# Column sums, stores and a last stage in block products: a transformer block in split fp32

## The chip, the cores and the metric

The kernel runs on one core of a Trainium2 chip. The time is that of the device for one execution, in microseconds (us). The engines are TensorE (PE in the rows; PEld its loading of weights), VectorE (DVE), ScalarE (ACT), GpSimd (POOL) and SyncE (SP). A name with a q at its end (SPq, POOLq) is an engine's own sequencer, which issues DMAs in order.

## What is computed

One layer of a transformer block for 512 tokens of width 2048, all in fp32:

```python
sh_a, sc_a, g_a, sh_f, sc_f, g_f = jnp.split(jax.nn.silu(c) @ ada_w[l] + ada_b[l], 6, axis=-1)
h = modulate(rms_norm(x, norm_mix[l]), sh_a, sc_a)
proj = h @ w_in[l]
...
x = x + g_a[:, None, :] * (jnp.concatenate([y_conv, y_attn], axis=-1) @ w_out[l])
h = modulate(rms_norm(x, norm_ffn[l]), sh_f, sc_f)
x = x + g_f[:, None, :] * ((jax.nn.silu(h @ ffn_w1[l]) * (h @ ffn_w3[l])) @ ffn_w2[l])
```

y_conv is a short convolution over three slices of proj, y_attn an attention over compressed, selected and near keys. The feed forward is 5632 wide, 44 blocks of 128. The vectors of the first line are 2048 long each; shift, scale and gate of the feed forward are its last three.

## The kernel before

**Numbers.** Each fp32 operand is split in a rounded part (hi, by a copy on ScalarE) and a remainder (lo, by a subtraction on VectorE), and a product is three matmuls: hi by lo, lo by hi, hi by hi (mm3, L96). A block of weights is loaded by SyncE, split, and then multiplied.

**The order.** The program is written as steps, and a scheduler places the instructions on each engine by it; woven generators (weave, L102) put steps of one work between steps of another. An engine runs its row in order, and so does a queue of DMAs.

**Column sums.** ada (L169) makes 512 columns of silu(c) @ ada_w: 16 pieces of the matrix, 128 x 512 (256 KB) each, are loaded by SyncE into a ring, and VectorE adds each, scaled, to acc (L185, one instruction of 128 x 512 a piece). ada_cols (L188) turns the sum into a column for shift or scale. In the token blocks (203 to 317 us) no sum is made. Beside the convolutions (317 to 700) ffn_cols (L792) makes six of the eight columns of the feed forward, one behind each convolution, out of a ring of two pieces. In the w_out stage (700 to 860; four column blocks n, L842) the ring has three buffers of two pieces; there stand, each in one piece, the sums of g_a for n + 1 and the last two columns. The gate of the feed forward, four rows, is made by gate_rows (L1106) inside the up stage: its loads are on GpSimd's queue, its sums (L1116) on VectorE, one step each third product.

**x2.** The result of w_out plus x is stored to memory as xd (L859), and read back in the end.

**Up stage** (920 to 1823 us). Each of 44 blocks u of 128 hidden columns: the first two plain, the other 42 as seven block products instead of eight (Strassen's method in Winograd's form; a product is 8 matmuls 512 wide, L922, and 8 of 256, L924). blocks (L894) loads four weight blocks by SyncE and, for the sum of two of them, loads the first again into t (or t2) and lets an accumulating DMA on GpSimd's queue add the second. More sums are made on VectorE (L1011). more and take (L929, L933) bring products together in d. The finished block is stored to memory (gd) by GpSimd (store, L974). begin starts the loads of a block five products ahead of its first.

**Down stage** (from 1823 us). Forty of the 44 hidden blocks in four groups b of ten, again as seven products of five units j, each unit 12 matmuls 512 wide (L1255). k_load (L1171) reads hidden blocks back on GpSimd's queue; a_parts (L1176) sums and splits them (ghi L1203, glo L1204); w_load (L1209) loads weights some units ahead, w_sum makes the sums for products 6 and 4 on VectorE (L1232, L1234), w_split splits (L1240), evict (L1258) adds products to y2. The last four blocks come as a plain tail (L1313 to the end): y2 times gate, plus xd, then 192 matmuls, and per tile a multiply, an add and a store.

Of the kernel before, what the change touches and what calls it, by code (L numbers as in the profile page):

```python
# [17 lines left out]
P = 128  # L18
# [51 lines left out]
def block_kernel(ctx: ExitStack, tc: tile.TileContext, a: dict, out: bass.AP):  # L70
# [98 lines left out]
    def ada(ring, width, c0, n, bias=False):  # L169
# [16 lines left out]
        return acc  # L186
# [203 lines left out]

    qk = ExitStack()
# [112 lines left out]
    def compress():  # L504
        per = cpool.tile([CMP_BLOCK, 2, HD], F32, name="per")
# [51 lines left out]
        b1 = cpool.tile([P, 256], F32, name="b1")  # L557
        hid = cpool.tile([P, 256], F32, name="hid")
# [21 lines left out]
        hrep = cpool.tile([P, 2, R, 32], F32, name="hrep")  # L580
        nc.gpsimd.memset(hrep, 0.0)
        for g in range(NKV):
# [4 lines left out]
            for h in range(2):  # L587
                nc.tensor.matmul(pv[:, :HD], hrep[:, h].rearrange("p r n -> p (r n)"), cw2[:, 1, h, :],
                                 start=h == 0, stop=h == 1)
# [20 lines left out]
    weave(token_blocks(), before_attention(), 1.5)  # L610
# [179 lines left out]
    wring = pool("aring", 2, stack=at_)  # L790

    def ffn_cols(ring_, width, j):  # L792

        m, j = 1 - j % 2, j // 2
        ada_cols(aux, ada(ring_, width, (3 + m) * D + j * 512, 512), 1, m, 4 * j, 4)

    def convs():
        for c in range(8):
            yield from conv(c)
            if c < 6:  # L800
                ffn_cols(wring, 512, c)
# [41 lines left out]
    for n in range(4):  # L843
# [3 lines left out]
        ada_bcast(aux, ga, acc_g)  # L847
        if n < 3:
            acc_g = ada(aring, 1024, 2 * D + (n + 1) * 512, 512, bias=True)
        pst = [main() for _ in range(NT)]  # L850
        for _ in token_block(w_out, n * 512, yT, every[8:] + every[:8], pst):
            pass
# [6 lines left out]
        nc.gpsimd.dma_start(xd[n], x2s[n])  # L859
        if n < 3:  # L860
            if n < 2:
                ffn_cols(aring, 1024, 6 + n)
            x2_turned(n)
# [88 lines left out]
    def h_sums(step):  # L952
# [15 lines left out]
        elif step == 4 * PLAIN - 1:  # L968
            h_parts(3, A[0, 1], 0, HK)
            hst.close()  # L970
            zone[1] = pool("raw2", 8, stack=ust, side="right")

    def store(f, g):
        (nc.gpsimd if f + 1 < NU else nc.scalar).dma_start(gd[f], g)  # L974
# [92 lines left out]

    order, late = [], None
# [37 lines left out]
    def gate_rows():  # L1106

        acc, raw = (accp.tile([P, 512], F32, tag="acc", name="acc") for _ in range(2))
        for n in range(4):
            c0 = 5 * D + n * 512  # L1110
            nc.gpsimd.memset(acc, 0.0)
            nc.gpsimd.dma_start(acc[0:1, :], a["ada_b"][:, c0:c0 + 512])
            for k in range(KC):
                nc.gpsimd.dma_start(raw, ada_v[:, k, c0:c0 + 512])
                yield
                nc.vector.scalar_tensor_tensor(acc, raw, cT[:, k:k + 1], acc, op0=ALU.mult, op1=ALU.add)  # L1116
            ps = aux()
            nc.tensor.matmul(ps[0:1, :], ones[:, 0:1], acc, start=True, stop=True)
            nc.scalar.copy(raw[0:1, :], ps[0:1, :])
            nc.gpsimd.dma_start(gfd[:, n * 512:(n + 1) * 512], raw[0:1, :])  # L1120

    gate = gate_rows()
# [8 lines left out]
    for n, s in enumerate(order):  # L1131
# [3 lines left out]
        if n + 5 < len(order):  # L1135
            begin(order[n + 5]["u"])
# [3 lines left out]
        if n >= 4 * PLAIN and n % 3 == 0:  # L1140
            next(gate, None)
# [9 lines left out]
    GC, HN = 5, D // 2  # L1151
    NG = FF // P // (2 * GC)
    tail = range(NG * 2 * GC, FF // P)
    PRODUCTS = (1, 5, 6, 3, 7, 2, 4)
    krp = pool("kraw", 1)
    gpp = pool("gparts", 3)
    ep = pool("e", 1)
    wz = pool("wz", 6)
    tz = pool("tz", GC)
    yp = pool("y2", 1)  # L1160
    y2 = yp.tile([P, NT, D], F32, name="y2")
    gf = yp.tile([P, D], F32, name="gf")
    tp = pool("tmp2", 2)
    kraw, W, A_, bank = {}, {}, {}, {}

    def k_load(b, half):

        fs = tail if b == NG else range((2 * b + half) * GC, (2 * b + half + 1) * GC)
        t = kraw[b, half] = krp.tile([P, GC, S], F32, tag=f"k{half}", name=f"k{half}")
        for j, f in enumerate(fs):  # L1170
            nc.gpsimd.dma_start(t[:, j, :], gd[f])  # L1171
# [6 lines left out]
    def a_parts_(b, p):  # L1178
        n = GC
# [100 lines left out]
    for n in range(-10, 0):  # L1280
        loads(n)
# [76 lines left out]
```

## Time and profile before

| | us |
|---|---|
| median of the runs (2299.56 to 2306.39) | 2303.61 |
| the profiled execution | 2297.38 |
| its span | 2295.6 |
| TensorE busy | 2197.4 |
| VectorE busy | 1758.1 |
| ScalarE busy | 989.5 |

The page gives busy time, the granted clock of TensorE (PEclk, 1.00 is full speed), the waits (engine line waited for: us, times, longest) and the chain that ended last. A wait names the engine that idled, its line and what released it. Lines are those of the kernel before; in the changed kernel they lie some 38 to 45 lower.

### The profile page before, as it was taken

To read this page: it belongs to the slowest core of one execution; us is meant where nothing else is said; L and a number is where in the kernel's file an instruction comes from. 1 tells how busy PE (TensorE), PEld (TensorE's weight loads), DVE (VectorE), ACT (ScalarE), POOL (GpSimd) and SP (SyncE) were. 2 spreads that over 40 slices of the span, in tenths; PEclk is the share of its full clock that TensorE was granted. 3 is DMA by queue.
4 is the path that set the end of the run, shared out by engine and by line. 5 is a ranking of instruction groups with operands and counts; after the bars stand their busy time and mean duration, and the time that the engine had idled before them with its cause. 6 is when DMAs were issued, how large, how long until landed. Compare 5 with 4: busy or idle time off the path is not lost. (4 is left out here: it accounts for less than half of the span.)

```text
span 2295.6 us, 30548 instructions
## 1 busy us (share of the span) xinstructions
PE 2197.4 (96%) x11401; PEld 1822.9 (79%) x11401; DVE 1758.1 (77%) x2577; ACT 989.5 (43%) x1554; POOL 263.9 (11%) x358
## 2 busy tenths in 40 slices
PE   7999999999999998999999999999999899999998
PEld 5788778787788776878888888888888777787776
DVE  6878478877756764968778788887878668888988
ACT  5235244555443232634444444444444354444441
POOL 5410000000000001010111111111010111101101
PEclk9999999999999999999999999999999999999999
DMA  9964455544435866397777777877776489576644
GB/s 325 363 215 135 158 180 168 173 127 143 120 118 202 277 231 179 112 217 170 181 201 182 196 193 198 214 183 179 175 175 157 160 250 266 164 219 215 168 136 160
DMA packets 432353, 435.20 MB, mean 190 GB/s; under 512 B 18132, under 2 KB 345016, under 8 KB 431052
## 3 DMA queue, kind: packets, MB, share of 16 engines
q1 hardware_dynamic: 358236, 303.38, 42.4%
q0 software_dynamic: 73824, 129.60, 23.5%
q8 instruction: 89, 1.46, 0.2%
q14 instruction: 60, 0.49, 0.1%
q10 hardware_dynamic: 144, 0.26, 0.0%
HBM read 413.25 MB, written 19.93 MB: 189 GB/s over the span
## 5 line engine op out<-in xcount | busy, mean ns | idle before, releaser
L910 ACT CAST whi<-raw 128x1024 fp32r<-128x1024 f32 x280 | 292.8, 1048 | 306.7 <-PE main L922 132.3
L922 PE MATMUL main<-hC,whi 128*128 128x512 f32 x1408 | 356.9, 395 | 9.2 <-DVE d L933 5.2
L915 DVE TENSOR_TENSOR wlo<-raw,whi 128x1024 fp32r<-128x1024 f32 x260 | 315.6, 1217 | 47.2 <-ACT whi L910 45.7
L922 PEld LDWEIGHTS main<-hC,whi 128*128 128x128 f32 x1408 | 253.6, 189 | 60.0 <-DVE d L933 7.3
L922 PE MATMUL aux<-hC,whi 128*128 128x512 f32 x1072 | 273.7, 398 | 13.0 <-DVE d L933 13.0
L922 PEld LDWEIGHTS aux<-hC,whi 128*128 128x128 f32 x1072 | 195.4, 191 | 51.9 <-DVE d L933 14.8
L924 PEld LDWEIGHTS main<-hC,wlo 128*128 128x128 f32 x1408 | 192.0, 190 | 13.8
L924 PE MATMUL main<-hC,wlo 128*128 128x256 f32 x1408 | 196.2, 282 | 0.0
L92 ACT CAST whi<-raw 128x1024 fp32r<-128x1024 f32 (+2 forms) x92 | 87.9, 959 | 230.9 <-PE main L100 143.5
L98 PE MATMUL main<-alo,whi 128*128 128x512 f32 x448 | 180.1, 402 | 1.4 <-DVE alo L346 1.4
L185 DVE SCALAR_TENSOR_TENSOR acc<-araw,cT,acc 128x512 f32<-128x512 f32 x184 | 137.7, 749 | 55.2 <-DMA araw<-in_ada_w 49.9
L99 PE MATMUL main<-ahi,wlo 128*128 128x512 f32 x448 | 176.6, 394 | 0.0
L100 PE MATMUL main<-ahi,whi 128*128 128x512 f32 x448 | 176.2, 394 | 0.0
L910 ACT CAST whi<-t 128x1024 fp32r<-128x1024 f32 x102 | 107.2, 1052 | 126.5 <-PE main L1255 32.3
L924 PEld LDWEIGHTS aux<-hC,wlo 128*128 128x128 f32 x1072 | 147.5, 192 | 11.1 <-DVE wlo L915 0.4
L98 PE MATMUL main<-wlo,ahi 128*128 128x512 f32 x384 | 152.7, 398 | 1.7 <-DVE t L856 1.6
L924 PE MATMUL aux<-hC,wlo 128*128 128x256 f32 x1072 | 150.9, 284 | 0.0
L100 PE MATMUL main<-whi,ahi 128*128 128x512 f32 x384 | 150.7, 393 | 0.0
L99 PE MATMUL main<-whi,alo 128*128 128x512 f32 x384 | 150.6, 392 | 0.0
L1011 DVE TENSOR_TENSOR raw<-raw 128x1024 f32<-128x1024 f32 x84 | 102.3, 1218 | 59.7 <-DMA raw<-in_ffn_w 59.5
L93 DVE TENSOR_TENSOR wlo<-raw,whi 128x1024 fp32r<-128x1024 f32 (+2 forms) x92 | 101.0, 1103 | 46.3 <-ACT whi L92 45.9
L1255 PE MATMUL main<-wlo,ghi 128*128 128x512 f32 x280 | 111.2, 399 | 14.0 <-ACT ghi L1203 7.4
(332 smaller groups left out, 4198.0 us busy)
## 6 DMA issues: line engine op xcount, KB each, us to landing
raw<-in_ffn_w SPq DMA_DIRECT2D x225, 512.0 KB, 5.0
w<-in_ffn_w SPq DMA_DIRECT2D x60, 512.0 KB, 5.2
araw<-in_ada_w POOLq DMA_DIRECT2D x56, 512.0 KB, 14.1
araw<-in_ada_w SPq DMA_DIRECT2D x112, 256.0 KB, 3.0
raw<-in_w_in SPq DMA_DIRECT2D x128, 192.0 KB, 2.7
t<-in_ffn_w SPq DMA_DIRECT2D x41, 512.0 KB, 6.4
t<-in_ffn_w POOLq DMA_DIRECT2D x41, 512.0 KB, 8.9
araw<-in_ada_w SPq DMA_DIRECT2D x40, 512.0 KB, 5.8
```

Source lines behind the costliest of these rows:

```text
L92: nc.scalar.copy(hi[:, :m], raw[:, :m])
L93: nc.vector.tensor_sub(lo[:, :m], raw[:, :m], hi[:, :m].bitcast(F32))
L98: nc.tensor.matmul(ps, lhs[0], rhs[1], start=first, stop=False)
L99: nc.tensor.matmul(ps, lhs[1], rhs[0], start=False, stop=False)
L100: nc.tensor.matmul(ps, lhs[0], rhs[0], start=False, stop=last)
L185: nc.vector.scalar_tensor_tensor(acc, w, s, acc, op0=ALU.mult, op1=ALU.add)
L910: nc.scalar.copy(hi, t)
L915: nc.vector.tensor_sub(lo, t, hi.bitcast(F32))
L922: nc.tensor.matmul(ps, wt[0][:, ks[k]], hC[p][:, k, :], start=first and k == 0, stop=False, skip_group_check=True)
L924: nc.tensor.matmul(ps[:, HS:], wt[1][:, ks[k]], hC[p][:, k, 0:HS], start=False, stop=last and k == HK - 1, skip_group_check=True)
L1011: nc.vector.tensor_add(to, x, y)
L1255: nc.tensor.matmul(ps[2 * t + c], x_[:, j, tok], w[:, cs], start=m == 0 and j == 0 and p in (1, 5, 2), stop=m == 2 and j == GC - 1 and p i ...
```

## The change

- **Column sums woven.** ada becomes a generator that gives way after each load. Twelve parts for the feed forward (eight columns of shift and scale, and the gate's four rows, ffn_part) are spread by beside: parts 0 to 2 in the token blocks (3.2 steps to one), 3 to 9 beside the convolutions (1.9), 10 and 11 in the last w_out block (2.5), and g_a's in the first three (1). gate_rows is gone from the up stage. Some tiles of the key compression share buffers, to make room for the ring.
- **x2 goes to the output.** It is stored to out itself, in pieces of 512 KB, and only tokens 256 to 511 of columns 0 to 1023 to xd.
- **Up stage.** Blocks are stored by SyncE in place of GpSimd; loads begin seven products ahead in place of five; five products before the end the second pool of weights (now its own stack) is closed, and the hidden blocks of the first down group are read.
- **Down stage.** All 44 blocks in block products, groups of 5, 6, 6, 5 units a product (22 units in each of seven products, no tail). The sum for product 4 is made by an accumulating DMA on GpSimd's queue, ten units ahead, the sum for product 6 by an add four units ahead; signs are turned in a_parts. In the last group finished blocks are scaled by the gate and added into out by six accumulating DMAs of 512 KB; the last product is done with xd, its last three units tile by tile.

The core of the diff:

```diff
-    def ada(ring, width, c0, n, bias=False):
+    def ada(ring, width, c0, n, got, bias=False):
...
                     nc.vector.scalar_tensor_tensor(acc, w, s, acc, op0=ALU.mult, op1=ALU.add)
-        return acc
+            yield
+        got.append(acc)
...
+    def ffn_part(ring_, width, j):
+
+        got = []
+        if j < 8:
+            m, j = 1 - j % 2, j // 2
+            yield from ada(ring_, width, (3 + m) * D + j * 512, 512, got)
+            ada_cols(aux, got[0], 1, m, 4 * j, 4)
+        else:
+            cs = slice((j - 8) * 512, (j - 7) * 512)
+            yield from ada(ring_, width, 5 * D + cs.start, 512, got, bias=True)
...
+            nc.gpsimd.dma_start(gfd[:, cs], got[0][0:1, :])
+        yield
...
-    weave(token_blocks(), before_attention(), 1.5)
+    early = ffn_parts(wring, 512, range(3))
+    weave(beside(token_blocks(), early, 3.2), before_attention(), 1.5)
...
+    later = ffn_parts(wring, 512, range(3, 10))
+    weave(beside(convs(), later, 1.9), attention_steps(), 0.68)
...
+        weave(token_block(w_out, n * 512, yT, every[8:] + every[:8], pst), side, 1 if n < 3 else 2.5)
...
-        nc.gpsimd.dma_start(xd[n], x2s[n])
+        for i in range(0, NT, 2):
+            to = xd[n] if n < 2 and i else \
+                out[0, i * P:(i + 2) * P, n * 512:(n + 1) * 512].rearrange("(i p) n -> p i n", p=P)
+            nc.gpsimd.dma_start(to, x2s[n][:, i:i + 2, :])
...
-        (nc.gpsimd if f + 1 < NU else nc.scalar).dma_start(gd[f], g)
+        (nc.sync if f + 1 < NU else nc.scalar).dma_start(gd[f], g)
...
-        if n + 5 < len(order):
-            begin(order[n + 5]["u"])
+        for m in (n + 6, n + 7) if n < 4 * PLAIN else (n + 7,):
+            if m < len(order) and (n >= 4 * PLAIN or m < 4 * PLAIN + 1):
+                begin(order[m]["u"])
...
-        if n >= 4 * PLAIN and n % 3 == 0:
-            next(gate, None)
+        if n == len(order) - 5:
+            zst.close()
+            krp = pool("kraw", 1, side="right")
+            for half in range(2):
+                k_load(0, half)
...
+        elif p == 4:
+            nc.gpsimd.dma_start(W[b, "t", j], block(1, 0), accum_op=ALU.add)
...
-            nc.vector.scalar_tensor_tensor(t, t, -1.0, W[b, 22, j], op0=ALU.mult, op1=ALU.subtract)
-        elif p == 4:
-            nc.vector.tensor_sub(t, W[b, 21, j], t)
+            t = W[b, "t", j]
+            nc.vector.tensor_add(t, t, W[b, 22, j])
...
+                if last and p in (3, 7, 2):
+                    nc.vector.scalar_tensor_tensor(y, y, -1.0 if c else 1.0, gf[:, cs], op0=ALU.mult, op1=ALU.mult)
+            if last and p in (3, 7, 2):
+                i = 2 * r + t
+                nc.gpsimd.dma_start(out[0, i * P:(i + 1) * P, c * HN:(c + 1) * HN], y2[i][:, c * HN:(c + 1) * HN],
+                                    accum_op=ALU.add)
...
-    AHEAD = {1: 4, 5: 9, 6: 10, 7: 7, 2: 7}
+    AHEAD = {1: 4, 5: 9, 6: 6, 7: 7, 2: 6, 4: 10}
```

VectorE in the token blocks, before: the rotary embedding of queries and keys (L464 to L469, L460) and the remainders of weights (L93).

```order
L467 TENSOR_TENSOR rw<-q_106,Zq 128x4x64 x2
L460 RECIPROCAL rq<-rq 128x4
L464 TENSOR_TENSOR ru<-q_106,Cq 128x512 x2
L468 TENSOR_TENSOR ru<-ru,rw 128x512
L93 TENSOR_TENSOR wlo<-raw,whi 128x1024
L469 TENSOR_TENSOR ru<-ru,rq 128x512
L467 TENSOR_TENSOR rw<-q_106,Zq 128x4x64 x2
L468 TENSOR_TENSOR ru<-ru,rw 128x512
```

The same place with the change (those lines are now L497 to L506):

```order
L504 TENSOR_TENSOR rw<-q_106,Zq 128x4x64 x2
L185 SCALAR_TENSOR_TENSOR acc<-araw,cT,acc 128x512
L505 TENSOR_TENSOR ru<-ru,rw 128x512
L185 SCALAR_TENSOR_TENSOR acc<-araw,cT,acc 128x512
L506 TENSOR_TENSOR ru<-ru,rq 128x512
L497 RECIPROCAL rq<-rq 128x4
L501 TENSOR_TENSOR ru<-q_106,Cq 128x512
L504 TENSOR_TENSOR rw<-q_106,Zq 128x4x64 x2
L93 TENSOR_TENSOR wlo<-raw,whi 128x1024
```

Behind nearly every step of the embedding, and ahead of the next remainder, there now stands a column sum (L185) that waits for its piece of ada_w.

GpSimd in the middle of the up stage, before: t and raw are the accumulating DMAs of weight sums, acc the gate's loads, gd the stores of hidden blocks.

```order
L905 DMA t_11514<-in_ffn_w 128x8x128
L1114 DMA acc<-in_ada_w 128x512 x2
L974 DMA gd_6515<-d_11328 128x512
L1114 DMA acc<-in_ada_w 128x512
L905 DMA raw<-in_ffn_w 128x8x128
L1114 DMA acc<-in_ada_w 128x512 x2
L974 DMA gd_6516<-d_11509 128x512
L1114 DMA acc<-in_ada_w 128x512
L905 DMA t_11878<-in_ffn_w 128x8x128
```

With the change GpSimd has only the sums there, and behind the last of them the reads of hidden blocks (k):

```order
L943 DMA raw<-in_ffn_w 128x8x128
L943 DMA t_15134<-in_ffn_w 128x8x128
L943 DMA raw<-in_ffn_w 128x8x128
L943 DMA t_15665<-in_ffn_w 128x8x128
L1115 DMA k_15922<-gd_6720 128x512
L1115 DMA k_15922<-gd_6721 128x512
L1115 DMA k_15922<-gd_6722 128x512
L1115 DMA k_15922<-gd_6723 128x512
```

The stores stand on SyncE's row in their place, between weight loads:

```order
L941 DMA raw<-in_ffn_w 128x8x128 x4
L941 DMA t_9470<-in_ffn_w 128x8x128
L1012 DMA gd_6725<-d_9170 128x512
L941 DMA raw<-in_ffn_w 128x8x128 x5
L1012 DMA gd_6726<-d_9347 128x512
L941 DMA raw<-in_ffn_w 128x8x128 x4
L941 DMA t_9824<-in_ffn_w 128x8x128
L1012 DMA gd_6727<-d_9524 128x512
L941 DMA raw<-in_ffn_w 128x8x128 x5
```

Each store stands behind the loads of t and five more of a later block; before, the same stretch of SyncE's row was weight loads alone, and the reads of k stood on GpSimd behind the last stores.

GpSimd from the up to the down stage, before:

```order
L974 DMA gd_6536<-d_15108 128x512
L905 DMA t_15467<-in_ffn_w 128x8x128
L974 DMA gd_6537<-d_15285 128x512
L974 DMA gd_6538<-d_15462 128x512
L974 DMA gd_6539<-d_15639 128x512
L1318 DMA r<-xd_6495 128x512 x2
L1171 DMA k_15973<-gd_6497 128x512
L1171 DMA k_15973<-gd_6498 128x512
```

Three stores and two reads of xd stood between the last sum (t) and the first k; with the change the first k follows that sum directly, as the rows above show.

More of the change, by code (lines that the diff above doesn't have):

```diff
@@ L388, in block_kernel, with ffn_parts, beside @@
     st0.close()
+    dram = ctx.enter_context(tc.tile_pool(name="spill", bufs=1, space=bass.MemoryType.DRAM))
+    gfd = dram.tile([1, D], F32, name="gfd")
+    wst = ExitStack()
+    wring = pool("aring", 2, stack=wst)
+    def ffn_part(ring_, width, j):
[7 more added lines that the diff above has]
+            yield from ada(ring_, width, 5 * D + cs.start, 512, got, bias=True)
+            ps = aux()
+            nc.tensor.matmul(ps[0:1, :], ones[:, 0:1], got[0], start=True, stop=True)
+            nc.scalar.copy(got[0][0:1, :], ps[0:1, :])
+            nc.gpsimd.dma_start(gfd[:, cs], got[0][0:1, :])
+        yield
+    def ffn_parts(ring_, width, js):
+        for j in js:
+            yield from ffn_part(ring_, width, j)
+    def beside(work, side, n):
+        due = 0.0
+        for _ in work:
+            due += n
+            while due >= 1:
+                next(side, None)
+                due -= 1
+            yield
     qk = ExitStack()
@@ L1065, in last_steps, with k_load @@
         return [p1, p5], [p6, p3, p7, p2, p4]
+    GS, GM, HN = (5, 6, 6, 5), 6, D // 2
+    NG = len(GS)
+    START = [2 * sum(GS[:b]) for b in range(NG)]
+    kraw = {}
+    def k_load(b, half):
+        n = GS[b]
+        t = kraw[b, half] = krp.tile([P, GM, S], F32, tag=f"k{half}", name=f"k{half}")
+        for j in range(n):
+            nc.gpsimd.dma_start(t[:, j, :], gd[START[b] + half * n + j])
     order, late = [], None
@@ L1104, in prepare @@
             s["lo"] = w_lo(s["o"]["b"][s["src"]], s["hi"])
[L1106 to L1122, printed above, removed]
     lead = {id(t): 3 if t["p"] != 4 else 2 if t is order[-1] else 5 for t in order}
@@ L1145, in block_kernel @@
     ust.close()
[L1151 to L1155, printed above, removed]
     gpp = pool("gparts", 3)
+    tz = pool("tz", GM)
+    wz = pool("wz", 6)
     ep = pool("e", 1)
[L1158 to L1171, printed above, removed]
+    yp = pool("y2", 3)
+    yq = pool("y3", 1, side="right")
+    y2 = [(yq if t == 3 else yp).tile([P, D], F32, tag="y", name="y") for t in range(NT)]
+    W, A_, bank = {}, {}, {}
     def a_parts(b, p):
@@ L1269, in block_kernel @@
[L1269 to L1280 removed]
+                cs = slice(c * HN + h * 512, c * HN + (h + 1) * 512)
+                y = y2[2 * r + t][:, cs]
@@ new lines, in last_tile @@
+    def last_tile(t, c):
+        cs = slice(c * 512, (c + 1) * 512)
+        y = y2[2 + t][:, cs]
+        u = accp.tile([P, 512], F32, tag="acc", name="acc")
+        nc.vector.tensor_mul(u, bank["x"][2 * t + c], gf[:, cs])
+        nc.vector.tensor_add(y, y, u)
+        nc.sync.dma_start(out[0, (2 + t) * P:(3 + t) * P, cs], y)
+    prods = [(b, p) for b in range(NG) for p in ((1, 5, 6, 3, 7, 2, 4) if b else (1, 2, 5, 6, 3, 7, 4))]
+    units = [(b, p, j) for b, p in prods for j in range(GS[b])]
@@ L1281, in block_kernel @@
+    AHEAD = {1: 4, 5: 9, 6: 6, 7: 7, 2: 6, 4: 10}
+    def loads(n):
+        for m in range(n + 13, n + 3, -1):
+            if 0 <= m < len(units):
+                b, p, j = units[m]
+                if (12 if (b, p) == (0, 5) else AHEAD.get(p)) == m - n:
+                    w_load(b, p, j)
+    for n in range(-13, 0):
         loads(n)
@@ L1337 @@
+        if last and p == 4:
+            if j == 0:
+                last_block()
+            if j < GS[b] - 3:
+                multiply(b, p, [j])
+            elif j == GS[b] - 1:
+                multiply(b, p, [j - 2, j - 1, j], last_tile)
+            continue
+        multiply(b, p, [j])
+        if j == GS[b] - 1:
+            evict(b, p)
 INS = ["x", "c", "positions", "ada_w", "ada_b", "norm_mix", "norm_ffn", "w_in", "conv_w", "cmp_pe_k", "cmp_k_w1",
```

228 lines of the change are left out of this document (106 added, 122 removed).

## Prediction

> **What bounds the kernel now.** I read the page first, then busy time by stage, then the waits of TensorE, then the rows of single lines. The page:
>
> ```profile
> span 2295.6 us, 30548 instructions
> PE 2197.4 (96%) x11401; PEld 1822.9 (79%) x11401; DVE 1758.1 (77%) x2577; ACT 989.5 (43%) x1554; POOL 263.9 (11%) x358
> ```
>
> TensorE (PE) is busy 96% of the span, so a gain comes from fewer matmuls, from the 98.2 us in which it is idle, or from matmuls that run slowly. Busy time by stage (window, its length, then busy us and instructions of each engine, clock, DMA share, GB/s) shows where it is idle:
>
> ```profile
> core 0: us, PE busy (x) PEld busy (x) DVE busy (x) ACT busy (x) POOL busy (x), PEclk, DMA share, GB/s
> 203.00:317.00 114.00, 112.28 (x561) 85.67 (x561) 64.97 (x155) 37.61 (x104) 0.00 (x0) 0.99 0.52 164
> 317.00:700.00 383.00, 381.21 (x1925) 307.14 (x1924) 287.00 (x585) 190.30 (x421) 1.06 (x2) 1.00 0.48 143
> 700.00:860.00 160.00, 151.87 (x665) 122.80 (x664) 113.09 (x145) 45.85 (x70) 3.75 (x7) 0.97 0.71 245
> 968.00:1020.00 52.00, 46.27 (x248) 40.08 (x247) 36.15 (x49) 19.68 (x29) 7.41 (x6) 0.93 0.99 224
> 1100.00:1550.00 450.00, 436.97 (x2448) 377.31 (x2447) 369.84 (x507) 199.03 (x288) 78.98 (x102) 1.00 0.77 194
> 1550.00:1800.00 250.00, 250.00 (x1434) 220.01 (x1433) 199.60 (x269) 115.31 (x166) 24.72 (x24) 1.00 0.67 164
> 1800.00:1900.00 100.00, 86.94 (x392) 70.52 (x391) 64.33 (x65) 47.26 (x58) 18.16 (x28) 0.94 0.75 232
> 1900.00:2205.00 305.00, 293.86 (x1268) 238.46 (x1266) 252.41 (x250) 138.32 (x131) 41.44 (x59) 0.99 0.71 207
> 2205.00:2250.00 45.00, 42.19 (x184) 34.12 (x184) 43.41 (x53) 16.67 (x16) 4.36 (x8) 1.00 0.28 94
> 2250.00:2295.60 45.60, 38.78 (x167) 30.74 (x165) 35.34 (x52) 5.28 (x5) 3.23 (x6) 0.99 0.47 159
> ```
>
> Token blocks (203 to 317) and convolutions (317 to 700) leave TensorE idle 1.7 and 1.8 us. The w_out stage leaves 8.1, the start of the up stage 5.7, the up stage 13.0 until 1550 and 0.0 behind that, and from 1800 on it is 13.1, 11.1, 2.8 and 6.8. What TensorE waited for, over the whole run (us, times, longest):
>
> ```profile
> PE aux L922 <- DVE d L933: 13.0, 7, 5.4
> PE aux L1255 <- DVE wlo L1240: 12.9, 11, 2.4
> PE main L1255 <- ACT ghi L1203: 7.4, 1, 7.4
> PE main L1255 <- DVE wlo L1240: 6.6, 8, 2.3
> PE aux L193 <- DVE acc L185: 6.4, 2, 3.9
> ```
>
> Nearly all of it is VectorE (DVE) being late: with up sums (L933), weight remainders (L1240), column sums (L185). The change works on these.
>
> **Fewer matmuls.** In steady work a 512 wide matmul of the down stage has this rate, and an up product these two pieces:
>
> ```profile
> 1911.62 13.60 PE aux L1255 x60
> 1700.05 1.84 PE main L922 x8
> 1701.89 0.95 PE main L924 x8
> ```
>
> 13.60 over 60 is 0.2267 us; an up product takes 2.79. The plain tail had 4 blocks, 4 columns, 4 token tiles and 3 passes, 192 matmuls; as two more units in each of seven products, 12 matmuls each, it is 168. 24 x 0.2267 = **5.4 us gained**.
>
> **The gate out of the up stage.** 64 sums of these leave it:
>
> ```profile
> L1116 DVE SCALAR_TENSOR_TENSOR acc<-acc,cT x64: 735/746/755, 865.1 to 1511.3; 128x512 f32<-128x512 f32 x64
> PE aux L922 <- DVE d L933: 7.7, 6, 2.5
> PE main L922 <- DVE d L933: 4.9, 7, 1.2
> ```
>
> The last two rows are TensorE's waits from 1100 to 1550: 12.6 of its 13.0 idle us. The last gate sum starts at 1511.3, and from 1550 to 1800 the same loop runs without them and without idle. I take that stretch as the model: 13.0 falls to 0.5, **12.5 gained**. Bounds: all 13.0, or only 5 if the longer lead of the loads and the stores, not the gate's absence, decide.
>
> **The start of the up stage and the slow clock.** Stalls cost twice, since the granted clock drops behind long ones. Three windows right behind stalls, and all from the last up product on:
>
> ```profile
> 1002.00:1010.00 8.00, 7.42 (x26) 6.32 (x27) 8.00 (x12) 2.58 (x4) 0.60 (x1) 0.62 0.58 165
> 1830.00:1835.00 5.00, 4.68 (x12) 3.38 (x13) 2.52 (x3) 0.95 (x3) 1.44 (x2) 0.59 1.03 420
> 1857.00:1862.00 5.00, 3.98 (x11) 3.19 (x12) 1.94 (x2) 2.00 (x2) 0.00 (x0) 0.66 1.04 352
> 1823.00:2295.60 472.60, 438.81 (x1872) 353.77 (x1872) 378.98 (x394) 196.72 (x195) 61.86 (x91) 0.98 0.67 203
> ```
>
> The first follows the wait of 5.4 us (DMA share 0.99 around it: the loads bunch). 26 matmuls take 7.42 us there; at an up product's 2.79 for 16 that is 4.5, so 2.9 are lost to the clock. The change begins a block's loads two products sooner and takes the gate's 256 KB loads out of this stretch; I expect 3 of the 5.4 + 2.9 to stay, **5 gained** (0 to 8). With waits of at most 2.5 us, 1100 to 1550 keeps clock 1.00. The Trainium skill, in "TensorE: Matmul & The Clock Gate", Part 1, puts the boundary at a window of about 3.4 us without work and half rate until about as long a busy one; the trace agrees on both sides of it, 2.5 and 5.4. By that page the stall of 4 us ahead of the last batch (below) would cost, as an estimate, 1.7 us more than I count; no row here is for a stall of 4 us.
>
> **The w_out stage.** The 6.4 us of waits for L185 come where 16 sums of a column stand in one piece; the changed order weaves one or two to a step, and columns go to earlier stages. Idle 8.1 falls to about 2: **6 gained** (2 to 8).
>
> **From the up to the down stage.**
>
> ```profile
> 1818.61 3.72 POOL L1171 DMA_DIRECT2D k<-gd  x7
> 1829.01 1.26 ACT L1203 CAST ghi<-k 128x1280 fp32r<-128x1280 f32 x1 [5.60 <-DMA k<-gd]
> ```
>
> The reads of the hidden blocks are issued from 1818.61 on; ScalarE gets them at 1829.01, and TensorE stands 7.4 us. Now five products earlier, 5 x 2.79 = 14 us: the reads have landed. Next late is the first remainder (glo), queued on VectorE behind a third weight remainder: about 2 us stay, 5 gained. The rest of 1800 to 1900, 13.1 less 7.4, is 5.7 of waits for L1240 while DMA is at 1.04; I leave 3.
>
> **The down stage.** VectorE is the late engine: 252 of 305 us busy, and its waits end on wlo. Leaving it is the fourth product's sum:
>
> ```profile
> L1234 DVE TENSOR_TENSOR t<-w,t x20: 1211/1216/1226, 1895.8 to 2218.4; 128x1024 f32<-128x1024 f32 x20
> ```
>
> 20 x 1.216 = 24.3 us, not to be added as such, since most lies beside matmuls: of 11.1 idle I leave 6. From 2205 on, 2.8 and 6.8 become 7: the plain tail goes, but four adds and four scalings are queued ahead of the last three units (some 4 us), and the multiply, add and store behind the last matmul stay. So 33.8 idle becomes 2 + 3 + 6 + 7 = 18, **15.8 gained** (5 to 24). And 438.81 busy us for 1872 matmuls are 14.4 over 1872 x 0.2267 = 424.4: the slow clock and refills behind those stalls. With fewer and shorter stalls I leave 6.4: **8 gained** (2 to 12).
>
> What replaces the sum is a DMA on GpSimd's (POOL) queue. Rows (median us from issue to landing):
>
> ```profile
> t<-in_ffn_w SPq DMA_DIRECT2D x41, 512.0 KB, 6.4
> t<-in_ffn_w POOLq DMA_DIRECT2D x41, 512.0 KB, 8.9
> araw<-in_ada_w SPq DMA_DIRECT2D x112, 256.0 KB, 3.0
> raw<-in_ffn_w SPq DMA_DIRECT2D x225, 512.0 KB, 5.0
> ```
>
> It is issued ten units ahead, 10 x 12 x 0.2267 = 27 us, against 8.9: hidden, at nothing, unless the queue is held (a rival below). The six transfers that add into the output in memory have no row; the last is issued some 5 units, 14 us, before the end and then has the 5 us of last stores too: nothing by the 8.9, up to 10 lost if they take three times that.
>
> **What the earlier stages lose.**
>
> ```profile
> L185 DVE SCALAR_TENSOR_TENSOR acc<-araw,cT,acc x184: 729/751/755, 299.4 to 840.5; 128x512 f32<-128x512 f32 x184
> DVE acc L185 <- DMA araw<-in_ada_w: 28.8, 37, 2.5
> ```
>
> 48 sums x 0.75 = 36 us go beside the token blocks: VectorE 65 + 36 = 101 of 114, and some of it lies in front of what TensorE waits for. I take **3 lost** (0 to 24). The convolutions get 16 more, 12 us on 287 of 383: **1 lost** (0 to 3).
>
> Sum: 5.4 + 12.5 + 5 + 6 + 15.8 + 8 - 3 - 1 = 48.7. The profiled execution, 2297.38, becomes 2248.7; it lies 6.2 under the median of the runs shown, so against 2303.61 I forecast **2255**.
>
> **Rivals.** First, the token blocks become bound by sums that wait for their loads. The second row above is the convolutions' own: 28.8 / 37 = 0.78 us a wait. If each of 48 sums waited so, 48 x (0.75 + 0.78) + 65 = 138 us of VectorE against 114, 24 in place of 3: 2276. For it: two buffers, 3.0 us a load, and 48 in 114 us. Against: in the convolutions only 37 waited. Chance 0.12.
>
> Second, the added DMAs come late, because GpSimd issues in order and stands in front of something else:
>
> ```profile
> POOL k L1171 <- DVE glo L1204: 125.6, 7, 34.2
> POOL gd L974 <- DVE d L1041: 341.5, 37, 18.6
> ```
>
> It stood up to 34.2 us at a reload of the hidden blocks. 34.2 against 27 ahead is 7 late, in three groups 21: 2276. Against it: the reloads move two units into their product, and the mean stand was 125.6 / 7 = 18. Chance 0.13. The Trainium skill, "DMA: Bandwidth & Descriptors", Anatomy of one DMA, has a fit that gives an estimate of 3.2 us for a transfer of 512 KB on this path, by which a late start would be made good sooner and I would say 0.08; the trace has 8.9, and the row decides.
>
> Third, slower than before: the hidden block's stores now stand on SyncE's queue, in front of weight loads. GpSimd stood 341.5 / 37 = 9.2 us at one, in a unit of 7 x 2.79 = 19.5. Loads are begun seven products ahead, 19.5, and a summed block needs 6.4 + 8.9 = 15.3: 4.2 us of slack. If SyncE stood as long, 5.0 would come through at each of 42 units; at half of that, 2.5, it is 105: 2360. It turns the result from 49 / 42 = 1.2 us a unit on. Against it: SyncE arrives later than GpSimd did, since each store stands behind five to ten loads that have their own waits. Chance 0.05.
>
> Fourth, more is gained: idle after 1800 falls to 8, and the refills to 2, 14 more: 2241. VectorE's relief would have to reach every stall. Chance 0.08.
>
> **How the numbers follow.** My forecast has 0.62. The range, **2238 to 2283**, takes in the fourth rival below and the first two above, with a spread of 7; the slower rival and both first ones together stay out. Two runs of this kernel differ by about 0.3%, 7 us. Faster by more: 0.62 + 0.12 + 0.13 + 0.08 less 0.04 for cases that add up: 0.91. Within it 0.04, slower 0.05.
>
> **What would show it.** Right: no idle TensorE from 1100 to the last up product; the wait for ghi gone and clock 1.00 behind it; L1240 waits of some 10 us in all; token blocks under 118 us. Wrong: waits of the kind acc <- araw beside the token blocks over 20 us; loads on SyncE behind a waiting gd; t of the fourth product landing after its unit begins; or matmuls still at 0.23 and more on average in the down stage without stalls.

## The result, and the profile after

The changed kernel takes 2263.31 us (median of 4 runs, 2262.73 to 2266.77), the kernel before 2304.07 (4 runs, 2299.56 to 2306.39): a ratio of 0.9829, 95% interval 0.9811 to 0.9847, 40.8 us less. 2255 was forecast, with a range of 2238 to 2283.

The page of the changed kernel:

```profile
span 2261.7 us, 30554 instructions
PE 2182.5 (96%) x11377; PEld 1812.0 (80%) x11377; DVE 1725.9 (76%) x2523; ACT 996.1 (44%) x1558; POOL 222.4 (10%) x267
```

The span is 33.9 us shorter than that of the profiled execution before, which lay some 7 us under its own median; the split below is of these 33.9. Busy time by stage, for windows that were shown of before, and for the down stage from its first matmul on:

```profile
core 0: us, PE busy (x) PEld busy (x) DVE busy (x) ACT busy (x) POOL busy (x), PEclk, DMA share, GB/s
203.00:317.00 114.00, 109.62 (x548) 81.56 (x547) 88.42 (x198) 34.72 (x91) 0.62 (x2) 0.99 0.74 241
317.00:700.00 383.00, 379.60 (x1913) 304.81 (x1912) 294.32 (x602) 189.57 (x431) 2.10 (x4) 1.00 0.52 154
700.00:860.00 160.00, 157.06 (x697) 126.89 (x695) 111.11 (x138) 49.92 (x76) 6.65 (x11) 0.99 0.72 248
...
968.00:1020.00 52.00, 49.03 (x271) 42.32 (x270) 37.66 (x51) 21.57 (x31) 6.17 (x4) 0.97 1.03 230
...
1100.00:1550.00 450.00, 450.00 (x2580) 396.05 (x2580) 361.05 (x484) 208.52 (x300) 35.48 (x23) 1.00 0.73 175
```

```profile
1792.40:2261.70 469.30, 433.11 (x1848) 348.37 (x1848) 343.02 (x339) 201.29 (x196) 79.75 (x106) 0.98 0.82 222
```

From 1100 to 1550 TensorE is not idle any more (13.0 us before). The w_out stage has 2.9 in place of 8.1, the token blocks 4.4 in place of 1.7, the convolutions 3.4 in place of 1.8. But from 1792.40 on TensorE stands idle for 469.30 - 433.11 = 36.2 us, more than in the same stretch before:

```profile
1830.30:2295.60 465.30, 438.81 (x1872) 353.77 (x1872) 377.75 (x393) 195.02 (x192) 60.25 (x88) 0.98 0.67 200
```

That is 465.30 - 438.81 = 26.5 us, and 7.4 us for ghi just ahead of it. What TensorE waited for there with the change (us, times, longest; L1282 is L1255 of before and L1262 its L1240, in the up stage L960 is L922 and L971 is L933, so lines of the down stage lie some 25 lower and not 38 to 45):

```profile
PE aux L1282 <- DVE wlo L1262: 16.2, 12, 3.7
PE main L1282 <- DVE wlo L1262: 14.7, 12, 4.7
...
PE main L1282 <- ACT ghi L1223: 1.7, 1, 1.7
```

Where a stage begins and ends is read from the rows of its matmuls (first and last start), here the up and the down stage of the changed kernel, and then of the kernel before:

```profile
L960 PE MATMUL main<-hC,whi x1408: 389/393/796, 916.5 to 1789.4; 128*128 128x512 f32 x176
L1282 PE MATMUL main<-wlo,ghi x308: 387/389/796, 1792.4 to 2242.5; 128*128 128x512 f32 x154
```

```profile
L922 PE MATMUL main<-hC,whi x1408: 387/393/797, 920.4 to 1821.6; 128*128 128x512 f32 x176
L1255 PE MATMUL main<-wlo,ghi x280: 389/389/797, 1830.3 to 2228.3; 128*128 128x512 f32 x140
```

| us | before | after | gained | forecast |
|---|---|---|---|---|
| up to the first up product | 920.4 | 916.5 | 3.9 | 6 - 3 - 1 = 2 |
| first to last up product | 901.2 | 872.9 | 28.3 | 12.5 + 5 = 17.5 |
| last up product to first down matmul | 8.7 | 3.0 | 5.7 | in the next |
| first down matmul to the end | 465.3 | 469.3 | -4.0 | with the one above 5.4 + 15.8 + 8 = 29.2 |
| span | 2295.6 | 2261.7 | 33.9 | 48.7 |

That the sum came out near is luck in part. The up stage gave 11 us more than forecast and the last two stretches together 27 us less; and of the 15 us that the split lacks, the medians show 8 (48.7 against 40.8), since the profiled execution before lay 7 us under its median. With 24 matmuls fewer the down stage became longer. That is what the experiments are for.

### The profile page after: what moved, and what is told of

It is laid out like the page before. It is cut to its first block, busy times and chain, and to the rows that moved or that the text cites. A ratio compares the mean times of both kernels' runs of the same rounds, so it can differ in the third digit from the quotient of the medians.

```text
span 2261.7 us, 30554 instructions
## 1 busy us (share of the span) xinstructions
PE 2182.5 (96%) x11377; PEld 1812.0 (80%) x11377; DVE 1725.9 (76%) x2523; ACT 996.1 (44%) x1558; POOL 222.4 (10%) x267
## 4 chain that ended last, share of the span: by engine, by line
PE 73%; DMA 12%; DVE 11%; issue 2%; ACT 1%; POOL 0%; SPq 0%; DVEq 0%; ACTq 0%; POOLq 0%
PE main L960 14%; PE aux L960 10%; PE main L962 7%; PE main L98 6%; PE main L100 6%; PE main L99 6%; PE aux L1282 5%; PE aux L962 5%; DMA araw<-in_ada_w 5%; PE main L1282 5%; DMA w<-in_ffn_w 5%; DVE acc L185 2%; DVE wlo L1262 2%; PE aux L98 1%; DMA raw<-in_ffn_w 1%
## 5 line engine op out<-in xcount | busy, mean ns | idle before, releaser
L960 PE MATMUL main<-hC,whi 128*128 128x512 f32 x1408 | 356.7, 395 | 5.2 <-DVE hC L977 3.7
L960 PEld LDWEIGHTS main<-hC,whi 128*128 128x128 f32 x1408 | 255.1, 190 | 51.9 <-DVE hC L977 4.3
L960 PE MATMUL aux<-hC,whi 128*128 128x512 f32 x1072 | 270.1, 393 | 0.0
L185 DVE SCALAR_TENSOR_TENSOR acc<-araw,cT,acc 128x512 f32<-128x512 f32 x248 | 185.6, 748 | 73.2 <-DMA araw<-in_ada_w 60.2
L960 PEld LDWEIGHTS aux<-hC,whi 128*128 128x128 f32 x1072 | 193.7, 190 | 34.9
L948 ACT CAST whi<-t 128x1024 fp32r<-128x1024 f32 x108 | 113.5, 1052 | 152.7 <-PE aux L1282 42.1
L92 ACT CAST whi<-raw 128x1024 fp32r<-128x1024 f32 (+2 forms) x84 | 79.5, 949 | 207.0 <-PE main L100 138.6
L962 PEld LDWEIGHTS aux<-hC,wlo 128*128 128x128 f32 x1072 | 146.3, 190 | 12.4 <-DVE wlo L953 1.9
L1262 DVE TENSOR_TENSOR wlo<-w,whi 128x1024 fp32r<-128x1024 f32 x66 | 79.9, 1222 | 81.3 <-ACT whi L948 81.2
L1282 PE MATMUL aux<-wlo,ghi 128*128 128x512 f32 x308 | 123.1, 400 | 16.2 <-DVE wlo L1262 16.2
```

Source lines behind the costliest of these rows:

```text
L92: nc.scalar.copy(hi[:, :m], raw[:, :m])
L185: nc.vector.scalar_tensor_tensor(acc, w, s, acc, op0=ALU.mult, op1=ALU.add)
L948: nc.scalar.copy(hi, t)
L960: nc.tensor.matmul(ps, wt[0][:, ks[k]], hC[p][:, k, :], start=first and k == 0, stop=False, skip_group_check=True)
L962: nc.tensor.matmul(ps[:, HS:], wt[1][:, ks[k]], hC[p][:, k, 0:HS], start=False, stop=last and k == HK - 1, skip_group_check=True)
L1262: W["last"] = nc.vector.tensor_sub(lo, t, hi.bitcast(F32)).ins
```

## The experiments

Two questions: what in the change freed the up stage, and why the down stage gave nothing. All twelve kernels start from the changed kernel; "up" is the time from first to last up product, "down" that from the first down matmul to the end, both of the profiled execution; ratios are to the kernel before, timed beside.

| | ratio (95%) | median us | up | down |
|---|---|---|---|---|
| the change | 0.9829 (0.9811 to 0.9847) | 2263.31 | 872.9 | 469.3 |
| gate back in the up stage | 0.9964 (0.9950 to 0.9978) | 2298.59 | 901.5 | 472.6 |
| lead 5, stores on GpSimd | 0.9830 (0.9807 to 0.9853) | 2267.60 | 878.4 | 467.2 |
| product 4's sum on VectorE | 0.9834 (0.9814 to 0.9854) | 2268.27 | 871.6 | 468.8 |
| product 4's sum left out | 0.9768 (0.9752 to 0.9785) | 2252.17 | 875.6 | 454.0 |
| product 7's sum on VectorE | 0.9697 (0.9675 to 0.9719) | 2238.48 | 875.6 | 438.3 |
| product 7 six units ahead | 0.9842 (0.9826 to 0.9857) | 2269.54 | 875.6 | 465.9 |
| product 4's DMA plain | 0.9823 (0.9800 to 0.9846) | 2263.38 | 875.3 | 466.6 |
| first reads of k late | 0.9833 (0.9818 to 0.9849) | 2268.55 | 870.8 | 469.4 |
| seventh w buffer, eight ahead | 0.9785 (0.9759 to 0.9811) | 2257.22 | 875.1 | 457.8 |
| 7 on VectorE, product 2 eight ahead | 0.9681 (0.9656 to 0.9706) | 2230.18 | 871.2 | 434.6 |
| 7 on VectorE, 4 left out | 0.9710 (0.9691 to 0.9729) | 2238.34 | 875.5 | 438.4 |
| 7 and 4 on VectorE | 0.9741 (0.9724 to 0.9759) | 2245.65 | 872.2 | 450.1 |

### The gate back in the up stage

gate_rows is put back as it was in the kernel before, and the four gate parts leave the other stages:

```diff
-    later = ffn_parts(wring, 512, range(3, 10))
+    later = ffn_parts(wring, 512, range(3, 8))
...
-            ffn_parts(aring, 1024, (10, 11))
+            iter(())
...
+    gate = gate_rows()
     lead = {id(t): 3 if t["p"] != 4 else 2 if t is order[-1] else 5 for t in order}
...
+        if n >= 4 * PLAIN and n % 3 == 0:
+            next(gate, None)
```

> The changed kernel with the gate's 64 sums and their loads put back into the up stage as they were (a sum each third product, loads on GpSimd), the four gate parts gone from the convolutions and the last w_out block. Theory (the gate's sums on VectorE made the up products late): the up stage from its first to its last product, 872.9 us with the change and 901.2 before, comes back to 893 or more, with over 10 us of waits of TensorE for L971/L967; the total is some 10 to 20 us above 2263.3, since the earlier stages win back some of it. Rival (the longer lead of the loads and the stores on SyncE did it): the up stage stays under 880 and the total under 2264.

The up stage takes 901.5 us, before it took 901.2. TensorE waits again (us, times, longest):

```profile
PE aux L908 <- DVE dg L907: 12.2, 1, 12.2
...
PE main L960 <- DVE d L971: 8.6, 9, 1.9
PE aux L960 <- DVE d L971: 8.3, 7, 2.5
```

16.9 us of waits for L971, as expected; the total is 0.9964, some 31 us above the change, more than the 10 to 20 expected: the stages ahead win nothing back, the first up product starts at 920.2 (916.5 with the change). The first row belongs to it: with the gate's sums on VectorE ahead of the up stage, TensorE waits 12.2 us for the norm's L907 (10.0 before, 2.9 with the change).

### The lead and the stores back

```diff
-        (nc.sync if f + 1 < NU else nc.scalar).dma_start(gd[f], g)
+        (nc.gpsimd if f + 1 < NU else nc.scalar).dma_start(gd[f], g)
...
-        for m in (n + 6, n + 7) if n < 4 * PLAIN else (n + 7,):
-            if m < len(order) and (n >= 4 * PLAIN or m < 4 * PLAIN + 1):
-                begin(order[m]["u"])
+        if n + 5 < len(order):
+            begin(order[n + 5]["u"])
```

> The changed kernel with the loads of a block begun five products ahead again in place of seven, and the hidden blocks stored by GpSimd again; the gate stays out of the up stage. Theory (the gate's sums): the up stage stays within 5 us of 872.9, the total within 8 us of 2263.3. Rival (lead and stores): the up stage at 890 or more, the total at 2280 or more.

The up stage is 5.5 us longer, just over the 5 expected, and the ratio is that of the change. The stage has one long wait at its start, where the changed kernel stands idle for 3.0 us:

```profile
PE aux L960 <- DVE d L971: 8.0, 1, 8.0
```

So nearly all of the up stage's gain is the gate's absence; lead and stores together are worth the stall at its start.

### Product 4's sum: on VectorE, left out, plain

Three kernels, with these edits in turn:

```diff
-        elif p == 4:
+        elif p == 4 and b == 0:
             nc.gpsimd.dma_start(W[b, "t", j], block(1, 0), accum_op=ALU.add)
...
             nc.vector.tensor_add(t, t, W[b, 22, j])
+        elif p == 4 and b:
+            t = W[b, "t", j]
+            nc.vector.tensor_add(t, t, W[b, 21, j])
```

```diff
-        elif p == 4:
-            nc.gpsimd.dma_start(W[b, "t", j], block(1, 0), accum_op=ALU.add)
```

```diff
-            nc.gpsimd.dma_start(W[b, "t", j], block(1, 0), accum_op=ALU.add)
+            nc.gpsimd.dma_start(W[b, "t", j], block(1, 0))
```

> The changed kernel with product 4's sum made on VectorE (one add of 128x1024 from the block that product 2 has in SBUF) in the last three groups, 17 units; in the first group it stays a DMA. Theory (the down stage is held by DMAs, and each accumulating DMA of 512 KB keeps all 16 engines for about 2.5 us): the waits for L1262 behind 1900 fall from 19 to under 12 us and the total is 5 to 12 us below 2263.3, though VectorE gets 17 x 1.22 = 21 us more. Rival (VectorE is still what is late): the total is 5 to 15 us above it.

> The changed kernel without product 4's accumulating DMA and without any sum in its place, which leaves the second block out of product 4's weights. It takes the 22 transfers away and gives VectorE nothing. Theory (held by DMAs): 10 to 20 us below 2263.3, and DMA share from 1792 on falls from 0.81 to about 0.69. Rival (VectorE late, or the chain of loads too short): less than 4 us below it.

> The changed kernel with product 4's accumulating DMA replaced by a plain one of the same block into the same tile from the same queue, so the sum is left out and the bytes from memory stay. The down stage takes 469.3 us with the accumulating DMA and 454.0 without any. If the adding is what costs: 454 to 460. If the bytes and the place in the queue cost: 465 to 470. From the time of packets I expect it between, near 461, as an accumulating transfer has 4.8 us of engine time a MB and a plain one 2.7.

The down stage of the three, in this order, one fence for each kernel:

```profile
1792.00:2260.80 468.80, 434.22 (x1848) 350.29 (x1848) 362.55 (x356) 201.75 (x196) 65.41 (x89) 0.98 0.73 203
```

```profile
1795.30:2249.30 454.00, 429.27 (x1848) 348.75 (x1848) 343.00 (x339) 201.70 (x196) 61.05 (x84) 0.98 0.72 204
```

```profile
1795.70:2262.30 466.60, 433.30 (x1848) 349.81 (x1848) 343.00 (x339) 201.40 (x196) 72.61 (x106) 0.98 0.77 224
```

With the sum on VectorE the stage takes what it took with the DMA (468.8 against 469.3): neither theory's number. With the sum left out it takes 15.3 us less, as the first theory had it. With a plain transfer it takes 466.6, not the 461 that I expected but in the 465 to 470 of bytes and place in the queue: 12.6 of the 15.3 us are there without any adding, so the transfer itself is what costs. And the first two rows speak against my theory of full DMA engines: a share of 0.73 and of 0.72, and 14.8 us between them.

### Product 7's sum on VectorE

The stalls show what is late. The timeline of the changed kernel in the first group's product 7, one of GpSimd's accumulating DMAs for it and then the engines at its longest stall (start, length, engine and line; in brackets the idle time before it and what ended it):

```profile
1867.53 1.14 POOL L1237 DMA_DIRECT2D w<-in_ffn_w  x1
...
1881.76 1.04 ACT L948 CAST whi<-w 128x1024 fp32r<-128x1024 f32 x1 [7.38 <-DMA w<-in_ffn_w]
1882.84 1.23 DVE L1262 TENSOR_TENSOR wlo<-w,whi 128x1024 fp32r<-128x1024 f32 x1 [6.50 <-ACT whi L948]
...
1884.12 0.80 PE L1282 MATMUL main<-wlo,ghi 128*128 128x512 f32 x1 [4.70 <-DVE wlo L1262]
```

The stall is put down to VectorE's wlo, but VectorE had waited 6.5 us for ScalarE, and ScalarE 7.4 us for the transfer, which had been issued at 1867.53, 14 us sooner. The transfers of the w tiles in the down stage (median us to landing), first with the change, then before, then with product 4's transfers left out:

```profile
w<-in_ffn_w SPq DMA_DIRECT2D x66, 512.0 KB, 8.0
...
w<-in_ffn_w POOLq DMA_DIRECT2D x22, 512.0 KB, 11.0
```

```profile
w<-in_ffn_w SPq DMA_DIRECT2D x59, 512.0 KB, 5.2
...
w<-in_ffn_w POOLq DMA_DIRECT2D x20, 512.0 KB, 7.1
```

```profile
w<-in_ffn_w SPq DMA_DIRECT2D x66, 512.0 KB, 7.5
w<-in_ffn_w POOLq DMA_DIRECT2D x22, 512.0 KB, 8.6
```

Product 7's block comes by two transfers, one behind the other: by these medians 12.3 us before, 19.0 with the change and 16.1 without product 4's transfers (the SPq rows hold the loads of products 6 and 2 too). And SyncE can issue the first only when a w buffer is free: six are shared by the blocks of products 6 and 3, of 7, and of 2. When product 4's transfers come, the second group shows:

```profile
1936.40 0.85 POOL L1251 DMA_DIRECT2D t<-in_ffn_w  x1 [27.97 <-DVE wlo L1262]
...
1949.90 2.66 POOL L1251 DMA_DIRECT2D t<-in_ffn_w  x3
1962.16 0.83 POOL L1237 DMA_DIRECT2D w<-in_ffn_w  x1 [9.60 <-DVE wlo L1262]
```

The program lists them ten units ahead, but GpSimd issues the first at 1936.40, as soon as product 6 gives t back, some 70 us before ScalarE first reads it for product 4 (2006.74). The last of the six lands at 1965.5, beside product 7's first loads. So they were not late; they came early and landed beside product 7's loads.

The edit takes product 7's second transfer away, and the buffer too: the sum is made on VectorE in the tile that products 6 and 3 have used, with one plain load into the ring of product 1.

```diff
-            W[b, "t3", j] = get(wz, "w", block(0, 1), block(1, 1))
+            W[b, 12, j] = get(ring[0], "raw", block(0, 1))
...
+        elif p == 7:
+            t = W[b, "t3", j] = W[b, 22, j]
+            nc.vector.tensor_add(t, t, W[b, 12, j])
```

> The changed kernel with product 7's sum made on VectorE out of the block that products 6 and 3 already hold, plus one plain load; the 22 accumulating DMAs of product 7 are gone, product 4's stay. Theory (the weights of product 7 come late, since a plain transfer of 8.0 us and an accumulating one of 11.0 us follow each other in a lead of seven units, 19 us, of which two go to the split): the stalls of product 7 (7.5 us in the first group, 5.3 in the second) fall to under 2 us each, the down stage from its first matmul to the end, 469.3 us, comes to 455 or less, and the total is 10 us or more below 2263.3. Rival (any sum moved between VectorE and DMA costs the same, as product 4's did): within 5 us of 2263.3.

The down stage is 31 us shorter, and VectorE is busier by 24:

```profile
1799.90:2238.20 438.30, 425.26 (x1848) 348.29 (x1848) 367.11 (x361) 202.20 (x196) 61.20 (x84) 0.99 0.76 212
...
PE aux L1285 <- DVE wlo L1265: 7.0, 5, 3.3
...
PE main L1285 <- DVE wlo L1265: 0.9, 1, 0.9
```

Of 30.9 us of waits for wlo 7.9 are left; the longest, 3.3, is in the first group's product 2. The DMA share is 0.76, higher than in the kernel with product 4's sum left out (0.72), whose down stage is 15.7 us longer: the engines' rate is not the limit, the chain of product 7's loads is. How much of the 31 us belongs to the second transfer and how much to the buffer, this edit does not tell.

### The lead of product 7: shorter, and longer with a buffer

```diff
-    AHEAD = {1: 4, 5: 9, 6: 6, 7: 7, 2: 6, 4: 10}
+    AHEAD = {1: 4, 5: 9, 6: 6, 7: 6, 2: 6, 4: 10}
```

```diff
-    t2p = pool("t2", 1)
+    t2p = pool("t2", 1, stack=ust)
...
-    wz = pool("wz", 6)
+    wz = pool("wz", 7)
...
-    AHEAD = {1: 4, 5: 9, 6: 6, 7: 7, 2: 6, 4: 10}
+    AHEAD = {1: 4, 5: 9, 6: 6, 7: 8, 2: 6, 4: 10}
```

> The changed kernel with product 7's loads begun six units ahead in place of seven. Theory (their lead is too short): 2.7 us less lead brings 1 to 2 us more stall in each group's product 7 at several units, the down stage is 8 us or more above 469.3. Rival (DMA engines are full, so the order decides nothing): within 3 us of 469.3.

> The changed kernel with a seventh buffer for the w tiles (its place comes from the t2 tile, given back with the up stage) and product 7's loads begun eight units ahead in place of seven. Theory (the two transfers of product 7's weights, one behind the other, are bound to start only when a block of product 3 gives its buffer back, too late by some us): one unit more of lead, 2.7 us, takes most of the stalls of up to 1.6 us away, the down stage comes from 469.3 to 460 or less, the total to 2256 or less. Rival (the DMA engines' rate is the limit): the down stage stays within 3 us of 469.3.

A unit less of lead changes nothing (465.9 against 469.3), which is against the theory of the lead as I put it; a unit more, with a buffer for it, takes 11.5 us away (the total, 2257.2, is just over the 2256 expected):

```profile
1801.60:2267.50 465.90, 432.65 (x1848) 349.28 (x1848) 343.04 (x339) 201.56 (x196) 79.79 (x106) 0.98 0.82 224
```

```profile
1796.60:2254.40 457.80, 430.35 (x1848) 349.21 (x1848) 343.33 (x339) 201.59 (x196) 79.67 (x106) 0.98 0.83 228
```

The two agree with a start that is set by the buffer's release, not by the number of units ahead: a load that is listed one unit earlier stands on SyncE's queue until the buffer comes. SyncE's own waits with the change fit it:

```profile
SPq L1235 <- DVE wlo L1262: 290.9, 87, 36.2
```

This line issues every plain load of the stage, not product 7's alone, and before it waited as long (310.8 us). A seventh buffer without the longer lead, and the longer lead without the buffer, were not run.

The second kernel moves 228 GB/s, more than the changed kernel's 222, so here too the rate was not the limit.

### On top of product 7's sum: product 2's lead, product 4 left out, product 4 on VectorE

The first of the three adds to the edit for product 7:

```diff
-    AHEAD = {1: 4, 5: 9, 6: 6, 7: 7, 2: 6, 4: 10}
+    AHEAD = {1: 4, 5: 9, 6: 6, 7: 7, 2: 8, 4: 10}
```

> Product 7's sum on VectorE as in the kernel of that experiment (2238.5 us, down stage 438.3), and product 2's loads begun eight units ahead in place of six. The one long stall left there, 3.3 us at the third unit of product 2 in the first group, should go: 2 to 6 us below 2238.5. If the loads of the first group come at the rate of the DMA engines, whatever their order, no change within 2 us.

> Product 7's sum on VectorE, and product 4's sum left out altogether (the second block is missing from its weights). Leaving product 4's transfers out took 15 us from the down stage while product 7's sum was a DMA. Theory (they cost only because product 7's two transfers were late already and got later beside them): with product 7's sum on VectorE, leaving them out gains less than 4 us on 438.3. Rival (the DMA engines' rate, or GpSimd's queue, is a cost of its own): 10 us or more.

> Both sums on VectorE (product 4's in the last three groups): VectorE gets 17 x 1.22 = 21 us more on 367 of 438, the DMAs 17 fewer. Theory (with product 7's transfers gone, DMAs no longer hold the stage, VectorE does): 2 to 12 us above 2238.5. Rival (DMAs still hold it): 2 us or more below.

Their down stages:

```profile
1794.20:2228.80 434.60, 423.50 (x1848) 347.10 (x1848) 366.87 (x361) 202.53 (x196) 61.26 (x84) 1.00 0.76 213
```

```profile
1799.20:2237.60 438.40, 424.25 (x1848) 346.80 (x1848) 367.00 (x360) 202.17 (x196) 42.11 (x62) 1.00 0.61 185
```

```profile
1791.90:2242.00 450.10, 429.86 (x1848) 349.62 (x1848) 385.44 (x378) 202.19 (x196) 46.50 (x67) 0.98 0.63 187
```

With product 2's loads eight units ahead the down stage is 3.7 us shorter and the stall of 3.3 us is gone, as expected; by the times it is 0.9681 against 0.9697, whose intervals overlap. It is the fastest kernel of this study, 2230.18 us. Leaving product 4's transfers out gains nothing now (438.4 against 438.3, at a DMA share of 0.61 against 0.76), where it gained 15.3 before: they cost only by making product 7's transfers later. Product 4's sum on VectorE makes the down stage 11.8 us longer and the median time 7.2, as the theory had it. VectorE is at 385 of 450 there, and the blocks of product 2 are held longer in the w buffers as well. The trace points at VectorE: behind the first group, each of TensorE's four waits of over 1 us (1.7, 1.4, 2.8 and 1.2) is for a wlo ahead of which VectorE was not idle. No run keeps the two apart.

### The first reads of the hidden blocks late

```diff
-            for half in range(2):
-                k_load(0, half)
         s["mm"](s)
...
     W, A_, bank = {}, {}, {}
+    for half in range(2):
+        k_load(0, half)
```

> The changed kernel with the reads of the first group's hidden blocks issued where the down stage begins, as before, in place of five products sooner. Theory (the prediction's transition term): the gap from the last up product's end to the first down matmul grows from 1.7 to 6 us or more, the stretch behind it runs at a lower clock, the total is 5 to 10 us above 2263.3. Rival (the loads of the down stage, which also wait for their buffers, are what is late): within 3 us of it.

The gap from the last up product to the first down matmul stays at 2.9 us (3.0 with the change), but this says nothing on the theory: the reads start at 1756.4 here and at 1756.2 with the change, since nothing else stands on GpSimd's row there. In the kernel with the stores back on GpSimd the gap is 3.0 too; the reads start at 1770.0 there, one store in front of them, still 28 us ahead of the last up product. So the stores alone do not bring the gap back. What remains of the change is the pool for the reads, which is opened five products before the end; that it is the cause was only argued.

## Why the prediction was right, and where it was not

- **The gate: right in mechanism, half its size.** 13.0 us of idle time went, 12.5 were forecast, and the stretch from 1550 to 1800 was the right model. But the up stage gained 28.3. From the first to the last up product, before and with the change:

```profile
920.40:1821.60 901.20, 882.32 (x4959) 767.48 (x4960) 731.13 (x973) 414.72 (x590) 126.47 (x153) 0.99 0.71 177
```

```profile
916.50:1789.40 872.90, 869.89 (x4951) 764.01 (x4952) 701.94 (x923) 413.34 (x586) 68.58 (x51) 0.99 0.70 171
```

Idle time fell from 18.9 to 3.0 us, and busy time by 12.4. Of these 12.4, 4.1 are the gate's own eight matmuls (L1118, from 1114.2 to 1540.0), which now stand ahead of the up stage: they moved, and were not gained. The other 8.3 are matmuls that take less time where TensorE does not wait. I had counted the slow clock only behind stalls of 5 us and more, and took the mean clock of 1.00 from 1100 to 1550 as proof that shorter ones are free; so the sentence that the trace agrees at 2.5 us does not hold either (rows in the last section). With the gate back, all 28.6 us are back.
- **The start of the up stage and the norm.** From 968 to 1020 TensorE is idle for 3.0 us in place of 5.7, where I left 3 for idle time and slow matmuls together. 271 instructions in place of 248 fit in these 52 us; at 0.174 us each (450.00 over 2580) that is 4.0 us, for 5. That the norm waited 10.0 us for a VectorE with gate sums in its row I had not seen; 7 us of that went. Up to the first up product idle time fell by 7.1 us in all (45.5 to 38.4), but busy time rose by 3.2 (874.9 to 878.1), the gate's 4.1 among them: so 3.9 were gained.
- **The w_out stage, token blocks, convolutions: right.** 2.9 idle where I left 2; 2.7 and 1.6 lost where I took 3 and 1. The first rival (sums that wait beside the token blocks, 24 us) did not come.
- **From the up to the down stage: right,** 5.7 for 5, though the place in the program is not the whole reason: moved back there, the reads started as early.
- **The down stage: wrong.** 15.8 + 8 were forecast. The step that failed is the price of the transfer that replaces product 4's sum: "27 us, against 8.9: hidden, at nothing". Product 4's own block was early enough; but its transfers made product 7's later (11.0 us to landing against 8.6 without them), and with product 7's second transfer gone they cost nothing (438.4 against 438.3). I did not ask whose transfers they delay, nor when the buffers that product 7 needs come free. Of the 33.8 idle us that were to become 18, the change has 36.2 from the first down matmul and 1.7 ahead of it, and the busy time over 1848 x 0.2267 = 418.9 is 14.2, not 6.4. The sign that I had named, waits for the remainder of some 10 us in all, came out at 30.9.
- **"VectorE is the late engine": only half of it.** Before, seven of TensorE's 19 waits for wlo, 12.0 of 19.5 us, had product 4's sum in front of the wlo in VectorE's row, and that sum had itself stood 3.3 to 5.7 us waiting for a block. One of them:

```profile
1996.77 1.22 DVE L1234 TENSOR_TENSOR t<-w,t 128x1024 f32<-128x1024 f32 x1 [5.49 <-DMA w<-in_ffn_w]
1997.91 1.22 DVE L1240 TENSOR_TENSOR wlo<-w,whi 128x1024 fp32r<-128x1024 f32 x1
...
1999.18 0.50 PE L1255 MATMUL aux<-wlo,ghi 128*128 128x512 f32 x1 [2.10 <-DVE wlo L1240]
```

So taking that sum away was right, and these waits went with it; but already there a transfer was late, and VectorE's 252 of 305 us did not show it. With the change the late transfers are product 7's.
- **The rivals.** The second, that added transfers make the stage late, had the right kind of cause, with 2276 for its price, but the wrong place: not product 4's own block behind GpSimd's stand at the reloads, but product 7's two transfers. The third, stores that hold SyncE's loads, did not come: from 1020 us to the last up product TensorE has no wait. Nor did the fourth, idle time after 1800 down to 8 us. With product 7's sum on VectorE, another change than the one forecast, the down stage is 438.3, where the forecast's terms gave 465.3 + 8.7 - 29.2 - 3.0 = 441.8.

## What to carry to other kernels

A wait that ends on VectorE is not yet VectorE's: follow it back, through VectorE's own row and the engine ahead of it, to the first idle time and what ended it, before a gain is booked for taking work from VectorE. A transfer that is itself early enough still costs what it does to the transfers beside it; here it was product 7's, which come in two steps and share six buffers, that felt it. And work that makes TensorE wait often and briefly is worth moving for more than the waits add up to: in the up stage idle time fell by 15.9 us, and the matmuls that stayed there took 8.3 us less.

## What the runs showed of the hardware

- Matmuls behind a stall of 2 to 2.5 us ran slowly in some cases and not in others. Before, behind a wait of 2.53 us, eight matmuls took 3.44 us in place of the 1.84 they take in steady work:

```profile
1205.66 3.44 PE L922 MATMUL aux<-hC,whi 128*128 128x512 f32 x8 [2.53 <-DVE d L933]
```

The granted clock of the 3 us behind it was 0.58, and behind a wait of 2.15 us, where eight matmuls took 2.11 us, it was 1.00 (the number ahead of DMA share and GB/s):

```profile
1205.60:1208.60 3.00, 2.94 (x8) 2.32 (x9) 3.00 (x5) 0.00 (x0) 0.54 (x1) 0.58 0.18 45
1374.70:1377.70 3.00, 2.98 (x17) 2.64 (x18) 3.00 (x4) 0.00 (x0) 0.00 (x0) 1.00 0.17 48
```

In the same kernel it was 0.50 behind a wait of 2.44 us, 0.63 behind 2.30 and 1.00 behind 2.10. Over 450 us such a drop does not show: the mean from 1100 to 1550 was 1.00.

- Accumulating transfers kept the DMA engines longer for a byte, but that decided little here. In the down stage of the changed kernel (packets, MB, share of 16 engines) q0 carries GpSimd's, the accumulating ones and the reads of hidden blocks, and q1 the others:

```profile
q0 software_dynamic: 13088, 46.67, 47.4%
...
q1 hardware_dynamic: 16496, 58.86, 33.6%
```

That is 1.02% a MB against 0.57%, 1.8 times as much. With product 4's 22 transfers plain in place of accumulating, and the same bytes, q0 holds them for 41.4% in place of 47.4%; but the stage took 466.6 us in place of 469.3.
